# Convolution taps and softmax exponentials tied to later places in a hybrid decoder layer

## The chip, the cores and the metric

The kernel runs on one core of a Trainium2 chip. The metric is device microseconds from the start to the end of one execution; lower is better.

## The reference

One decoder layer, 256 tokens of width 1024, in fp32, up to the final norm:

```python
hn = rmsnorm(h, mix_norm_g[l])
conv_a, conv_b, q, k_c, v_c, ... = split(hn @ w_in[l])
y_conv = conformer_conv(conv_a, conv_b, ...)   # a*sigmoid(b), 31-tap causal depthwise conv, layernorm, silu
y_nsa  = nsa_mixer(q, k_c, v_c, ...)           # compressed, selected and window attention, gated
h = h + concat([y_conv, y_nsa]) @ w_out[l]
h = h + memory_attention(rmsnorm(h, ...), rmsnorm(mem, ...), ...)
h = h + peer(rmsnorm(h, ...), ...)             # product keys: top 16 of 128 x 128 experts, 8 heads
return rmsnorm(h, final_norm_g)
```

In `peer`, each token takes per head the 16 best of 16,384 experts, a softmax over their scores gives the gates, and the output is the sum over experts of gate x gelu(h . u) x v.

## The kernel before

**Engines.** PE (TensorE) multiplies. An fp32 product is made of three: each weight chunk of 128 x 1024 comes by DMA from SP's queue into `raw` (4 buffers), ACT rounds each half of it to `hi` (line 137), and DVE or POOL subtracts to get `lo` (line 138); lines 148 to 150 then multiply hi by the activations' high and low part, and lo by the high part, for 8 values of k: 24 matmuls per chunk. PE's instructions run in the order of the program text. The other engines' instructions were put in order by a list scheduler at build time; each engine works strictly through its own list. `tc.keep_in_program_order(t)`, which the change uses, forbids the scheduler to put instruction t ahead of anything written before it on the same engine; what is written behind t may still be moved ahead of it.

**First stretch (0 to 105 us).** Loop `for i in range(4)` projects the convolution's inputs, two weight chunks for each i (`pb`, `pa`). The first norm's scale is a sum over the channels (`r0`), put into a row by `r0.rows()` (matmul `sr_x`, line 224, then ACT's `rs_x`). `conv_in` scales, gates and writes `u[:, i]`, and appends the 31 taps of channel block i to a list; `conv(n)` takes n taps off the list and writes them into the program. One tap (lines 271 and 273) is one DVE instruction on 128 x 256, accumulating into `yc[:, i]`: 124 in all. Then come the compressed keys' and values' projections (`pkv`), the queries and keys (`pq`, with their rotation on DVE and ACT, `rope`), and the values (`pv`), with conv(3) after each chunk. Then PE works on the memory's keys (`pmk`, line 442), whose matmuls `fill` doles out as filler for the attention.

**Attention loop (`for n in range(18)`, 100 to 183 us).** Each n issues the scores of a unit of heads (`pss`), filler matmuls (`pmk`, then `pmv`), the transposes of unit n-2 (`ptt`), and conv(6). On DVE a unit is a row maximum (`amx`, lines 562 and 563), a reciprocal and a product (`asm`, 568 and 569) and a scaling (`ape`, 574). At n = 0 `cmp_keys` writes `kcT` (500, 501). At n = 12 `ln_mean` writes the remaining taps and adds up the four blocks into `lsum` (610 to 613); at n = 13 `ln_center` multiplies it with ones (`pmu`, 619) and subtracts (621).

**Experts (317 to 1107 us).** DVE works down a chain of top-16 searches (lines 901 to 953) for two halves of the tokens: scores, candidates, the softmax's inputs `ge` (928), and the experts' indices `ix` (953), which the gate matrices need. Beside it PE multiplies with all 128 chunks of u (`u_chunk`, result `pu`), ACT writes their gelu: the first J = 36 into `slA` (999), the others into `slB`. POOL splits the weights (`lo`) for i < J, DVE for the others. `choice_gates` at i = J - 12 = 24 has, for each half, the exponential of `ge` (ACT, 962; it needs another activation table than gelu, so a table load stands ahead of it, and another ahead of the next gelu), the sums `gs`, their reciprocal, and the product `gt` (964 to 967). `picked_out` transposes indices and gates at i = 30 to 35. From chunk 36 on, `gates4` (64 times) makes gate columns of four tokens on DVE and PE and multiplies them in (lines 1012 to 1024). Then line 1072 accumulates Y over all 128 chunks of v, from 759 us on.

Of the kernel before, what the change touches and what calls it, by code (L numbers as in the profile page):

```python
# [9 lines left out]
F32 = mybir.dt.float32  # L10
# [5 lines left out]
AF = mybir.ActivationFunctionType  # L16
ALU = mybir.AluOpType
# [3 lines left out]
P = 128  # L21
T = 256
D = 1024
KC = 8
# [68 lines left out]
def build(tc, A, out, dbg=None):  # L93
    nc = tc.nc
    V, S, G, PE = nc.vector, nc.scalar, nc.gpsimd, nc.tensor
# [17 lines left out]
    def Pm(name):  # L113
        return par[:, PC[name][0]:PC[name][1]]
# [28 lines left out]
    def wchunk(src, engs=None, width=P):  # L143

        return wsplit(wload(src), engs, width)
# [6 lines left out]
    def proj(ps, w, x, ks=range(KC)):  # L152
        for k in ks:
            mm3(ps, w[k], x[0][:, k], x[1][:, k], k == 0, k == KC - 1)
# [20 lines left out]
    def psum(w, name, tag="mm"):  # L175
        return pm.tile([P, 512], F32, name=name, tag=tag, bufs=4)[:, :w]
# [70 lines left out]
    hx = (hx_h, hx_l)  # L247
# [11 lines left out]
    u = ch.tile([P, 4, 30 + T], F32, name="u")  # L259
    V.memset(u[:, :, 0:30], 0.0)  # L260
    yc = ch.tile([P, 4, T], F32, name="yc")
    taps = []

    def conv(n):
        for _ in range(min(n, len(taps))):
            taps.pop(0)()

    def tap(i, j):
        w = Pm("conv_w")[:, i * TAPS + j:i * TAPS + j + 1]
        if j == 0:  # L270
            V.tensor_scalar(yc[:, i], u[:, i, 0:T], w, Pm("conv_b")[:, i:i + 1], op0=ALU.mult, op1=ALU.add)
        else:
            V.scalar_tensor_tensor(yc[:, i], u[:, i, j:j + T], w, yc[:, i], op0=ALU.mult, op1=ALU.add)  # L273

    def conv_in(i, pb, pa):
        tb = wk.tile([P, T], F32, name=f"tb{i}", tag="tb")
        V.tensor_mul(tb, pb, r0.row)
        th = wk.tile([P, T], F32, name=f"th{i}", tag="th")
        S.activation(th, tb, AF.Tanh, scale=0.5)
        ta = wk.tile([P, T], F32, name=f"ta{i}", tag="ta")  # L280
        V.scalar_tensor_tensor(ta, pa, 0.5, r0.row, op0=ALU.mult, op1=ALU.mult)
        V.scalar_tensor_tensor(u[:, i, 30:], th, 1.0, ta, op0=ALU.add, op1=ALU.mult)
        for j in range(TAPS):
            taps.append(lambda j=j: tap(i, j))

    pend = []
    for i in range(4):
        pb = psum(T, f"pb{i}")
        wb = wchunk(A["w_in_t"][2 * i]) if i else w0
        proj(pb, wb, hx, range(4))  # L290
        if i == 1:
            r0.sums()
        proj(pb, wb, hx, range(4, KC))
        wa = wchunk(A["w_in_t"][2 * i + 1], None)
        if i == 0:
            for k in range(KC):
                r0.add(xT[:, k])
            nc.sync.dma_start(con1, A["con"][:, 0:NCON1])
        pa = psum(T, f"pa{i}")
        proj(pa, wa, hx, range(6))  # L300
        if i == 1:
            r0.rows()
            conv_in(*pend)
        proj(pa, wa, hx, range(6, KC))
        if i == 0:
            pend = (i, pb, pa)
        else:
            conv_in(i, pb, pa)
        conv(6)
    nc.sync.dma_start(con2, A["con"][:, NCON1:])  # L310
    posi = wk.tile([P, T], I32, name="posi", tag="rt")
    nc.sync.dma_start(posi, A["pos"].partition_broadcast(P))
# [31 lines left out]
    for i in range(2):  # L344
        G.memset(KV[i], 0.0)
        ps = psum(T, f"pkv{i}")
        proj(ps, wchunk(A["w_in_t"][8 + i]), hx)
        kvT = wk.tile([P, T], F32, name=f"kvT{i}", tag="kvT")
        V.tensor_mul(kvT, ps, r0.row)
        kt = KV[i]  # L350
        S.activation(kt[0:64, 0, 0:T], kvT[0:64, :], AF.Copy)
        S.activation(kt[64:128, 1, 0:T - 1], kvT[64:128, 1:T], AF.Copy)
        nc.sync.dma_start(kt[64:128, 0, 0:T - 1], kvT[0:64, 1:T])
        nc.sync.dma_start(kt[0:64, 1, 0:T], kvT[64:128, :])
        V.tensor_copy(kt[:, 2, 0:32:2], Pm("cmp_pos")[:, 16 * i:16 * i + 16])
        conv(3)
    nc.sync.dma_start(w2, A["w2"])

    w1 = [mp.tile([P, 16, P], F32, name=f"w1_{i}", tag=f"w1_{i}") for i in range(2)]
# [31 lines left out]
    for i in range(6):  # L391
        dst = kraw[i] if i < 2 else qraw[:, i - 2]
        ps = psum(T, f"pq{i}")
        proj(ps, wchunk(A["w_in_t"][10 + i]), hx)
        V.tensor_mul(dst, ps, r0.row)
        if i >= 2:
            nc.sync.dma_start(w1[i // 2 - 1][:, 8 * (i % 2):8 * (i % 2) + 8], A["w1"][i // 2 - 1, :, 8 * (i % 2):8 * (i % 2) + 8])
        if i == 1:
            rm.sums()
        todo.append((i, dst))  # L400
        if i > 1:
            rope(*todo.pop(0))
        conv(3)


    vn = ch.tile([P, 2, 256], F32, name="vn")
# [1 line left out]
    for w in range(4):  # L408
        wc = wsplit(wload(A["w_in_v"][w], 560), (V, V), 280, 280)
        for j in range(2):  # L410
            k = 2 * w + j
            for hf in range(2):
                sl = slice(hf * P, (hf + 1) * P)
                PE.matmul(pv[hf], hx_h[:, k, sl], wc[j][0], start=(k == 0), stop=False)
                PE.matmul(pv[hf], hx_h[:, k, sl], wc[j][1], start=False, stop=False)
                PE.matmul(pv[hf], hx_l[:, k, sl], wc[j][0], start=False, stop=(k == KC - 1))
        if w % 2:
            rope(*todo[w // 2])
        if w == 1:
            rm.rows()  # L420
        conv(3)
    gate = ch.tile([P, 2, 8, 3], F32, name="gate")
    chalf = wk.tile([P, 2], F32, name="chalf", tag="bcol")
    V.tensor_scalar(chalf, r0.col, 0.5, None, op0=ALU.mult)
# [210 lines left out]
    for n in range(18):  # L635
        if n < 16:
            scores(*units[n])
        if n == 17:
            wc0 = wchunk(A["w_out"][0])
        fill(7 if n < 4 else 5 if n < 14 else 6)  # L640
        if n == 0:
            cmp_keys()
        if n == 1:
            cmp_values()
            cmp_scores(0)
        if n == 2:
            cmp_scores(1)
            prs = psum(512, "prsel", "at")
            for k in range(4):
                PE.matmul(prs[:, k * P:(k + 1) * P], C("rsel")[0:64, k * P:(k + 1) * P], vc2, start=True, stop=True)  # L650
            V.tensor_copy(vcp, prs.rearrange("p (a b) -> p a b", a=4))
        if n in (4, 5):
            cmp_transpose(n - 4)
        if n >= 6 and (n - 6) % 4 == 0:
            weighted((n - 6) // 4)
        if n >= 2:
            transposes(*units[n - 2])
        conv(6)
        if n == 12:
            lsum = ln_mean()  # L660
        if n == 13:
            ln_center(lsum)
        if n == 15:
            rc.sums()
        if n == 16:
            rc.rows()
            ln_out()
# [32 lines left out]
    for i in range(2, KC):  # L700
        ps = psum(T, f"pwo{i}")
# [118 lines left out]
    for i in range(2, KC):  # L820
        ps = psum(T, f"pmw{i}")
# [27 lines left out]
    for i in range(16):  # L849
        ps = psum(T, f"ppq{i}")  # L850
# [16 lines left out]
    hn_h = h2p.tile([P, KC, T], F32R, name="hn_h", tag="act_h")  # L867
    hn_l = h2p.tile([P, KC, T], F32R, name="hn_l", tag="act_l")
# [9 lines left out]
    pp = outer.enter_context(tc.tile_pool(name="pp", bufs=1, space=PSUM, **RW))  # L878
# [17 lines left out]
    for hf in range(2):  # L896
        top = tp.tile([P, 16, 16], F32, name=f"top{hf}", tag="top")
        tix = tp.tile([P, 16, 16], U32, name=f"tix{hf}", tag="tix")
        for hp in range(16):
            s = sco[hf][:, hp]  # L900
# [58 lines left out]
    def choice_gates():  # L959
        for hf in range(2):  # L960
            ge = picked[hf][2]
            S.activation(ge, ge, AF.Exp)
            gs = tp.tile([P, 8], F32, name=f"gs{hf}", tag="gs")
            V.tensor_reduce(gs, ge, axis=AX.X, op=ALU.add)
            V.reciprocal(gs, gs)
            gt = picked[hf][2] = tp.tile([P, P], F32, name=f"gt{hf}", tag=f"gt{hf}")
            V.tensor_tensor(gt.rearrange("p (k h) -> p h k", h=8), ge, gs.unsqueeze(2).to_broadcast([P, 8, 16]), op=ALU.mult)
            show(f"g_{hf}", gt)

    def picked_out(hf, j):  # L970

        sl = slice(hf * P, hf * P + P)
        pt = pp.tile([P, 512], F32, name=f"ptk{hf}{j}", tag="w", bufs=2)[:, 0:P]
        PE.transpose(pt, picked[hf][j], C("ident"))
        if j < 2:
            S.activation((i1T, i2T)[j][:, sl], pt, AF.Copy)  # L976
        else:
            S.activation(gTh[:, sl], pt, AF.Copy, scale=GSC)
            V.scalar_tensor_tensor(gTl[:, sl], pt, GSC, gTh[:, sl], op0=ALU.mult, op1=ALU.subtract)


    J = 36
    e1 = outer.enter_context(tc.tile_pool(name="e1", bufs=1, side="left", **RW))
    slA = e1.tile([P, J, T], F32, name="slA")
    tmp = outer.enter_context(tc.tile_pool(name="tmp", bufs=2, side="left", **RW))
# [1 line left out]
    V.tensor_copy(iota2, C("iota").unsqueeze(2).to_broadcast([P, P, 2]))  # L987

    def u_chunk(i):
        ps = pp.tile([P, 512], F32, name=f"pu{i}", tag="w" if i < J - 8 and i % 4 > 1 else "s", bufs=2)[:, 0:T]  # L990
        proj(ps, wchunk(A["u"][i], (G, G) if i < J else (V, V)), (hn_h, hn_l))
        return ps

    for i in range(J):
        if i == J - 12:
            choice_gates()
        if i >= J - 6:
            picked_out((i - J + 6) // 3, (i - J) % 3)
        S.activation(slA[:, i], u_chunk(i), AF.Gelu_apprx_tanh)
    tk_st.close()  # L1000
    e2 = outer.enter_context(tc.tile_pool(name="e2", bufs=1, side="right", **RW))
# [170 lines left out]
```

## Time and profile before

| | |
|---|---|
| median of 3 runs | 1117.01 us (1116.13 to 1117.02) |
| profiled execution | 1117.35 us, of which the span of the trace is 1115.6 |
| PE busy | 1069.5 us, 96% of the span, 7362 matmuls |
| DVE, ACT, POOL busy | 882.1 us (79%), 590.1 us (53%), 111.2 us (10%) |
| mean granted TensorE clock | 0.983 of full speed |
| chain that ended last | PE 87%, DVE 5%, issue 4%, POOL 2%, ACT 2% |

Times are counted from the span's start. A row of a timeline gives the start, the duration, the engine, the line, the operation with output<-inputs, and in brackets how long the engine had stood idle and whose end released it. A row that ends in x3 is three like instructions in a row, and its duration reaches from the first's start to the last's end. Durations overlap a little: an instruction's successor can start before its last result is written, so start-to-start distances are what a queue costs. "PEclk" or granted clock is the share of full speed (2.4 GHz) that TensorE was granted in a stretch; 0.5 is 1.2 GHz.

### The profile page before, as it was taken

To read this page: it belongs to the slowest core of one execution; us is meant where nothing else is said; L and a number is where in the kernel's file an instruction comes from. 1 tells how busy PE (TensorE), PEld (TensorE's weight loads), DVE (VectorE), ACT (ScalarE), POOL (GpSimd) and SP (SyncE) were. 2 spreads that over 40 slices of the span, in tenths; PEclk is the share of its full clock that TensorE was granted. 3 is DMA by queue.
4 is the path that set the end of the run, shared out by engine and by line. 5 is a ranking of instruction groups with operands and counts; after the bars stand their busy time and mean duration, and the time that the engine had idled before them with its cause. 6 is when DMAs were issued, how large, how long until landed. Compare 5 with 4: busy or idle time off the path is not lost.

```text
span 1115.6 us, 20623 instructions
## 1 busy us (share of the span) xinstructions
PE 1069.5 (96%) x7362; PEld 980.5 (88%) x7362; DVE 882.1 (79%) x2229; ACT 590.1 (53%) x1354; POOL 111.2 (10%) x86
## 2 busy tenths in 40 slices
PE   8889999999999849999999999999999999999997
PEld 7878778999999749999999999998888888888885
DVE  7998857988789995788899999996666666666665
ACT  5722456666446335566555555455555555555554
POOL 0000000000037749300000000000000000000000
PEclk9899999999999969999999999999999999999999
DMA  8633224625434415644545454456555556665662
GB/s 279 201 107 103 76 95 139 219 97 171 153 114 151 152 57 189 194 164 154 170 155 167 155 170 163 160 170 209 189 195 196 193 190 193 199 193 191 194 198 80
DMA packets 51687, 182.47 MB, mean 164 GB/s; under 512 B 5760, under 2 KB 6528, under 8 KB 51456
## 3 DMA queue, kind: packets, MB, share of 16 engines
q1 hardware_dynamic: 51296, 180.62, 49.8%
q8 instruction: 58, 0.95, 0.3%
q10 hardware_dynamic: 288, 0.52, 0.1%
q14 instruction: 45, 0.37, 0.1%
HBM read 179.81 MB, written 1.05 MB: 162 GB/s over the span
## 4 chain that ended last, share of the span: by engine, by line
PE 87%; DVE 5%; issue 4%; POOL 2%; ACT 2%; DMA 0%; SPq 0%; POOLq 0%; ACTq 0%; DVEq 0%
PE Y L1072 31%; PE pu L148 10%; PE pu L150 10%; PE pu L149 10%; PE pmk L442 3%; POOL lo L138 2%; PE pmv L458 2%; PE pw L1018 1%; PE ppq L148 1%; PE ppq L149 1%; PE ppq L150 1%; PE pw L1019 1%; DVE lo L138 1%; PE pmw L149 1%; PE pmw L148 1%
## 5 line engine op out<-in xcount | busy, mean ns | idle before, releaser
L137 ACT ACTIVATE hi<-raw 128x512 fp32r<-128x512 f32 x632 | 379.2, 623 | 175.8 <-PE pu L149 61.5
L138 DVE TENSOR_TENSOR lo<-raw,hi 128x512 fp32r<-128x512 f32 (+1 forms) x560 | 370.4, 683 | 26.3 <-ACT hi L137 20.0
L148 PE MATMUL pu<-hn_h,hi 128*128 128x256 f32 x1024 | 296.3, 289 | 18.2 <-ACT hi L137 18.2
L150 PE MATMUL pu<-hn_h,lo 128*128 128x256 f32 x1024 | 291.7, 285 | 2.7 <-POOL lo L138 2.7
L149 PE MATMUL pu<-hn_l,hi 128*128 128x256 f32 x1024 | 290.2, 283 | 0.0
L148 PEld LDWEIGHTS pu<-hn_h,hi 128*128 128x128 f32 x1024 | 197.0, 192 | 18.4 <-ACT hi L137 18.4
L150 PEld LDWEIGHTS pu<-hn_h,lo 128*128 128x128 f32 x1024 | 196.7, 192 | 5.3 <-POOL lo L138 5.1
L149 PEld LDWEIGHTS pu<-hn_l,hi 128*128 128x128 f32 x1024 | 197.1, 193 | 0.0
L1072 PE MATMUL Y<-hi,al 128*128 128x512 f32 x512 | 158.1, 389 | 0.0
L1072 PE MATMUL Y<-hi,ah 128*128 128x512 f32 x512 | 158.1, 389 | 0.0
L1072 PE MATMUL Y<-lo,ah 128*128 128x512 f32 x512 | 158.0, 389 | 0.0
L1072 PEld LDWEIGHTS Y<-hi,al 128*128 128x128 f32 x512 | 96.1, 188 | 19.9
L1072 PEld LDWEIGHTS Y<-lo,ah 128*128 128x128 f32 x512 | 96.1, 188 | 19.9
L1072 PEld LDWEIGHTS Y<-hi,ah 128*128 128x128 f32 x512 | 96.0, 188 | 20.0
L158 DVE TENSOR_TENSOR al<-slB,ah 128x256 fp32r<-128x256 f32 x92 | 39.1, 425 | 89.9 <-PE Y L1072 89.9
L138 POOL TENSOR_TENSOR lo<-raw,hi 128x512 fp32r<-128x512 f32 x72 | 103.7, 1476 | 36.5 <-ACT hi L137 36.4
L157 ACT ACTIVATE ah<-slB 128x256 fp32r<-128x256 f32 x92 | 38.5, 418 | 115.7 <-PE Y L1072 115.7
L1024 ACT ACTIVATE slB<-pw 128x364 f32<-128x364 f32 (+31 forms) x64 | 33.4, 522 | 64.7 <-DVE slB L1023 54.2
L273 DVE SCALAR_TENSOR_TENSOR yc<-u,par,yc 128x256 f32<-128x256 f32 x120 | 56.0, 478 | 0.3
L158 DVE TENSOR_TENSOR al<-slA,ah 128x256 fp32r<-128x256 f32 x36 | 15.3, 425 | 33.6 <-PE Y L1072 33.6
L1012 DVE TENSOR_TENSOR o<-iota,i1T 128x512 f16<-128x512 f16 x64 | 28.6, 448 | 12.7 <-ACT i1T L976 12.7
L157 ACT ACTIVATE ah<-slA 128x256 fp32r<-128x256 f32 x36 | 15.0, 418 | 44.1 <-PE Y L1072 43.0
(387 smaller groups left out, 1786.7 us busy)
## 6 DMA issues: line engine op xcount, KB each, us to landing
raw<-u SPq DMA_DIRECT2D x128, 512.0 KB, 3.4
raw<-v SPq DMA_DIRECT2D x128, 512.0 KB, 4.3
raw<-peer_w_q SPq DMA_DIRECT2D x16, 512.0 KB, 3.3
raw<-w_in_t SPq DMA_DIRECT2D x15, 512.0 KB, 4.3
raw<-w_mem_k SPq DMA_DIRECT2D x8, 512.0 KB, 3.4
raw<-w_mem_v SPq DMA_DIRECT2D x8, 512.0 KB, 3.4
raw<-w_out SPq DMA_DIRECT2D x8, 512.0 KB, 3.5
raw<-w_mem_q SPq DMA_DIRECT2D x8, 512.0 KB, 4.3
```

Source lines behind the costliest of these rows:

```text
L137: S.activation(hi, r, AF.Copy)
L138: (engs or (V, V))[q].tensor_sub(lo, r, hi.bitcast(F32))
L148: PE.matmul(ps, w[0], xh, start=start, stop=False)
L149: PE.matmul(ps, w[0], xl, start=False, stop=False)
L150: PE.matmul(ps, w[1], xh, start=False, stop=stop)
L157: S.activation(dst[0], src, AF.Copy)
L158: V.tensor_sub(dst[1], src, dst[0].bitcast(F32))
L273: V.scalar_tensor_tensor(yc[:, i], u[:, i, j:j + T], w, yc[:, i], op0=ALU.mult, op1=ALU.add)
L442: PE.matmul(ps, wr[:, k * P:(k + 1) * P], mg[:, k], start=(k == 0), stop=(k == KC - 1))
L1012: V.tensor_tensor(o1, i4, over_i(i1T), op=ALU.is_equal)
L1024: S.activation(slB[:, done - J:, n0:n0 + 4].rearrange("p i n -> p n i"), pw[:, :, done:], AF.Copy, scale=1.0 / GSC)
L1072: PE.matmul(Y[nh][c], lhs[:, sl], wc[c][t], start=False, stop=i == KEYS - 1 and lhs is a[1], skip_group_check=True)
```

## The change

It has two parts. **Convolution:** each tap is tied behind all that is written before it on DVE. The first norm's row and the gating of channel blocks 0 and 1 move from chunk i = 1 (after six values of k) to i = 2 (after four). `pb0` and `pa0` go to the PSUM tag "at", so that they live until then. Fewer taps are written in the first stretch (conv(4), conv(2)) and more in the attention loop (conv(7)). **Experts:** the exponentials are tied behind all that ACT has been given so far; J goes from 36 to 40, so that `choice_gates` stands at chunk 32 rather than 24; POOL splits chunks 0 to 33 (JG = 34) and DVE from 34 on; `picked_out` runs two per chunk at 37 to 39 rather than one at 30 to 35. The gate groups are spread over the chunks from 40 on, up to chunk 125, as before.

```diff
@@ tap
-            V.tensor_scalar(yc[:, i], u[:, i, 0:T], w, Pm("conv_b")[:, i:i + 1], op0=ALU.mult, op1=ALU.add)
+            t = V.tensor_scalar(yc[:, i], u[:, i, 0:T], w, Pm("conv_b")[:, i:i + 1], op0=ALU.mult, op1=ALU.add)
         else:
-            V.scalar_tensor_tensor(yc[:, i], u[:, i, j:j + T], w, yc[:, i], op0=ALU.mult, op1=ALU.add)
+            t = V.scalar_tensor_tensor(yc[:, i], u[:, i, j:j + T], w, yc[:, i], op0=ALU.mult, op1=ALU.add)
+        tc.keep_in_program_order(t)
@@ for i in range(4)
-        pb = psum(T, f"pb{i}")
+        pb = psum(T, f"pb{i}", "mm" if i else "at")
...
-        pa = psum(T, f"pa{i}")
-        proj(pa, wa, hx, range(6))
-        if i == 1:
+        pa = psum(T, f"pa{i}", "mm" if i else "at")
+        proj(pa, wa, hx, range(4))
+        if i == 2:
             r0.rows()
-            conv_in(*pend)
-        proj(pa, wa, hx, range(6, KC))
-        if i == 0:
-            pend = (i, pb, pa)
+            for p in pend:
+                conv_in(*p)
+        proj(pa, wa, hx, range(4, KC))
+        if i < 2:
+            pend.append((i, pb, pa))
         else:
             conv_in(i, pb, pa)
-        conv(6)
+        conv(4)
@@ after each chunk of pkv, of pq and of pv
-        conv(3)
+        conv(2)
@@ for n in range(18)
-        conv(6)
+        conv(7)
@@ choice_gates
-            S.activation(ge, ge, AF.Exp)
+            tc.keep_in_program_order(S.activation(ge, ge, AF.Exp))
@@ experts
-    J = 36
+    J = 40
+    JG = 34
@@ u_chunk
-        ps = pp.tile([P, 512], F32, name=f"pu{i}", tag="w" if i < J - 8 and i % 4 > 1 else "s", bufs=2)[:, 0:T]
-        proj(ps, wchunk(A["u"][i], (G, G) if i < J else (V, V)), (hn_h, hn_l))
+        ps = pp.tile([P, 512], F32, name=f"pu{i}", tag="w" if i < J - 6 and i % 4 > 1 else "s", bufs=2)[:, 0:T]
+        proj(ps, wchunk(A["u"][i], (G, G) if i < JG else (V, V)), (hn_h, hn_l))
@@ for i in range(J)
-        if i == J - 12:
+        if i == J - 8:
             choice_gates()
-        if i >= J - 6:
-            picked_out((i - J + 6) // 3, (i - J) % 3)
+        if i >= J - 3:
+            for j in range(2):
+                picked_out((2 * (i - J + 3) + j) // 3, (2 * (i - J + 3) + j) % 3)
```

Line numbers of the changed kernel are one to four higher than those of the kernel before.

ACT's order in the experts, before, around the first exponential (`hi` is a rounding, `slA` a gelu; the row at line 999 with `pu_4522` is the gelu of chunk 3):

```order
L137 ACTIVATE hi_4597<-raw_4595 128x512
L137 ACTIVATE hi_4601<-raw_4595 128x512
L999 ACTIVATE slA<-pu_4486 128x256
L137 ACTIVATE hi_4633<-raw_4631 128x512
L137 ACTIVATE hi_4637<-raw_4631 128x512
L999 ACTIVATE slA<-pu_4522 128x256
L962 ACT_TABLE_LOAD
L962 ACTIVATE ge_4175<-ge_4175 128x128
L137 ACTIVATE hi_4669<-raw_4667 128x512
```

The second half's exponential stands in the same way behind the gelu of chunk 14. ACT's order now, around both (`pu_5530` is chunk 31; `raw_5651` is chunk 34's weights):

```order
L1003 ACTIVATE slA<-pu_5494 128x256
L137 ACTIVATE hi_5653<-raw_5651 128x512
L137 ACTIVATE hi_5657<-raw_5651 128x512
L1003 ACTIVATE slA<-pu_5530 128x256
L964 ACT_TABLE_LOAD
L964 ACTIVATE ge_4175<-ge_4175 128x128
L964 ACTIVATE ge_4367<-ge_4367 128x128
L137 ACTIVATE hi_5689<-raw_5687 128x512
L1003 ACT_TABLE_LOAD
L1003 ACTIVATE slA<-pu_5578 128x256
```

The exponentials moved from behind chunks 3 and 14 to behind chunk 31 and the roundings of chunk 34, and share two table loads instead of four.

DVE's order now at the end of the searches (`ix_4403` is the last of the chain, `raw_5651` again chunk 34's weights; before, no `lo` stood here, and chunk 36's came behind the first rows of the gate groups):

```order
L953 TENSOR_TENSOR ohx_4397<-ohx_4397 128x512
L953 TENSOR_TENSOR ohx_4397<-ohx_4397 128x256
L955 TENSOR_TENSOR ix_4403<-ohx_4397 128x128
L138 TENSOR_TENSOR lo_5654<-raw_5651,hi_5653 128x512
L138 TENSOR_TENSOR lo_5658<-raw_5651,hi_5657 128x512
L966 TENSOR_REDUCE gs_5567<-ge_4175 128x8
L967 RECIPROCAL gs_5567<-gs_5567 128x8
L969 TENSOR_TENSOR gt_5570<-ge_4175,gs_5567 128x8x16
L138 TENSOR_TENSOR lo_5690<-raw_5687,hi_5689 128x512
```

The first weights that DVE splits now stand behind its last search, with the sums of the gates behind them; the two sets of gs and gt rows stood inside the searches before.

DVE's order now at the end of the taps in the attention loop (`raw_1999` and `raw_2028` are the first two weight chunks of `w_out`):

```order
L576 TENSOR_SCALAR ape_1816<-ape_1816,asm_1817 128x256
L273 SCALAR_TENSOR_TENSOR yc<-u,par,yc 128x256 x2
L138 TENSOR_TENSOR lo_2002<-raw_1999,hi_2001 128x512
L273 SCALAR_TENSOR_TENSOR yc<-u,par,yc 128x256
L138 TENSOR_TENSOR lo_2006<-raw_1999,hi_2005 128x512
L273 SCALAR_TENSOR_TENSOR yc<-u,par,yc 128x256 x9
L138 TENSOR_TENSOR lo_2031<-raw_2028,hi_2030 128x512
L273 SCALAR_TENSOR_TENSOR yc<-u,par,yc 128x256
L138 TENSOR_TENSOR lo_2035<-raw_2028,hi_2034 128x512
L273 SCALAR_TENSOR_TENSOR yc<-u,par,yc 128x256 x6
L614 TENSOR_TENSOR lsum_1804<-yc 128x256
L615 TENSOR_TENSOR lsum<-lsum,lsum_1804 128x256
```

Between the second `kcT` row and this `lsum` row there are now 92 taps (before 36), 24 more rows of the attention's units, and four `lo` of `w_out` (before none). Ahead of the last rotation of the first stretch there are 30 taps (before 57), and between that and `kcT` two (before 31).

## Rows read from the trace of the kernel before

**Rows 1.** The page: parts 1 and 5 (busy, mean ns | idle before, releaser).
```profile
PE 1069.5 (96%) x7362; PEld 980.5 (88%) x7362; DVE 882.1 (79%) x2229; ACT 590.1 (53%) x1354; POOL 111.2 (10%) x86
...
L148 PE MATMUL pu<-hn_h,hi 128*128 128x256 f32 x1024 | 296.3, 289 | 18.2 <-ACT hi L137 18.2
...
L138 DVE TENSOR_TENSOR lo<-raw,hi 128x512 fp32r<-128x512 f32 (+1 forms) x560 | 370.4, 683 | 26.3 <-ACT hi L137 20.0
```

**Rows 2.** Timeline of ACT, 340 to 404 (start us, us, engine line op [idle before <-releaser]).
```profile
340.31 0.36 ACT L999 ACTIVATE slA<-pu 128x256 f32<-128x256 f32 x1
...
343.19 0.36 ACT L999 ACTIVATE slA<-pu 128x256 f32<-128x256 f32 x1
...
348.80 0.31 ACT L962 ACTIVATE ge<-ge 128x128 f32<-128x128 f32 x1 [3.95 <-DVE ge L928]
...
403.06 0.31 ACT L962 ACTIVATE ge<-ge 128x128 f32<-128x128 f32 x1 [23.77 <-DVE ge L928]
```

**Rows 3.** Timeline of PE, 384 to 410.
```profile
385.46 0.28 PE L150 MATMUL pu<-hn_h,lo 128*128 128x256 f32 x1
...
403.94 0.58 PE L148 MATMUL pu<-hn_h,hi 128*128 128x256 f32 x1 [18.20 <-ACT hi L137]
...
406.15 0.41 PE L150 MATMUL pu<-hn_h,lo 128*128 128x256 f32 x1
...
408.85 0.31 PE L148 MATMUL pu<-hn_h,hi 128*128 128x256 f32 x1
```

**Rows 4.** Windows: us; busy of PE, PEld, DVE, ACT, POOL; PEclk, DMA share, GB/s.
```profile
25.00:85.00 60.00, 50.83 (x360) 48.81 (x359) 56.39 (x155) 30.41 (x66) 0.00 (x0) 0.90 0.51 165
...
108.55:145.02 36.47, 36.47 (x201) 29.03 (x199) 32.50 (x111) 16.57 (x61) 0.00 (x0) 1.00 0.25 82
...
720.00:740.00 20.00, 20.00 (x184) 19.83 (x183) 20.00 (x45) 10.79 (x30) 0.00 (x0) 1.00 0.47 154
```

**Rows 5.** Timeline of PE, 43 to 90.
```profile
45.27 0.58 PE L150 MATMUL pkv<-hx_h,lo 128*128 128x256 f32 x1 [4.63 <-DVE lo L138]
...
84.87 5.34 PE L442 MATMUL pmk<-mg,raw 128*128 128x256 f32 x24
```

**Rows 6.** Timeline of DVE, 89 to 138, taps.
```profile
90.00 2.85 DVE L273 SCALAR_TENSOR_TENSOR yc<-u,par,yc 128x256 f32<-128x256 f32 x7
...
135.36 1.53 DVE L273 SCALAR_TENSOR_TENSOR yc<-u,par,yc 128x256 f32<-128x256 f32 x3
```

**Rows 7.** Timelines of DVE and PE, 108 to 165.
```profile
108.55 0.24 DVE L501 TENSOR_SCALAR kcT<-pkc,par 64x16 f32<-64x16 f32 x1
...
144.59 0.43 DVE L613 TENSOR_TENSOR lsum<-lsum,lsum 128x256 f32<-128x256 f32 x1
...
164.75 0.60 PE L619 MATMUL pmu<-lsum,ones 128*128 128x256 f32 x2
```

**Rows 8.** Timeline of POOL, 330 to 440.
```profile
336.94 7.92 POOL L138 TENSOR_TENSOR lo<-raw,hi 128x512 fp32r<-128x512 f32 x6 [0.93 <-ACT hi L137]
...
349.71 33.50 POOL L138 TENSOR_TENSOR lo<-raw,hi 128x512 fp32r<-128x512 f32 x22 [4.85 <-ACT hi L137]
```

**Rows 9.** Timeline of DVE, 403 to 467.
```profile
403.47 0.28 DVE L942 SCALAR_TENSOR_TENSOR pd<-pu,pu 128x128 f32<-128x128 uint32 x1
...
410.67 1.37 DVE L942 SCALAR_TENSOR_TENSOR pd<-pu,pu 128x128 f32<-128x128 uint32 x1
...
422.56 1.50 DVE L967 TENSOR_TENSOR gt<-ge,gs 128x128 f32<-128x128 f32 x1
...
430.65 1.27 DVE L953 TENSOR_TENSOR ix<-ohx 128x128 f32<-128x128 f16 x1
...
444.58 2.75 DVE L1012 TENSOR_TENSOR o<-iota,i1T 128x512 f16<-128x512 f16 x2 [12.65 <-ACT i1T L976]
...
466.13 0.42 DVE L1012 TENSOR_TENSOR o<-iota,i1T 128x512 f16<-128x512 f16 x1
```

**Rows 10.** Timeline of ACT, 429 to 470.
```profile
461.94 0.36 ACT L999 ACTIVATE slA<-pu 128x256 f32<-128x256 f32 x1
```

More of the change, by code (lines that the diff above doesn't have):

```diff
@@ L402, in build @@
             rope(*todo.pop(0))
-        conv(3)
+        conv(2)
     vn = ch.tile([P, 2, 256], F32, name="vn")
@@ L420, in build @@
             rm.rows()
-        conv(3)
+        conv(2)
     gate = ch.tile([P, 2, 8, 3], F32, name="gate")
```

## The prediction

> **What bounds the kernel now.** I read the page's busy shares first: PE is busy for 1069.5 of 1115.6 us, so a change can only win what PE loses at its few stops, and can lose whatever new stop it makes [rows 1]. The costliest stop is in the same part of the page: one wait of 18.2 us of the u multiplication for a rounding on ACT [rows 1]. The timeline of ACT tells why the rounding was late. ACT stood still for 3.95 us ahead of the first exponential and for 23.77 us ahead of the second, both for DVE's `ge`, with the roundings of later chunks queued behind [rows 2]. PE ran out of rounded weights at 385.46, resumed at 403.94, and its matmuls took 0.41 us instead of 0.28 until 408.85 [rows 3]. That is half-speed work, 1.2 instead of 2.4 GHz: 15 matmuls in 4.91 us, of which 0.8 went to two waits for POOL, against 1.8 at 0.12 each (24 take 2.88, the distance of two gelus [rows 2]). The aftermath of a long stop costs 2.3 us.
>
> Then the windows, for the stretches in which the taps lie. From 25 to 85 us DVE is busy for 56.39 of 60 us and PE for 50.83, at a mean clock of 0.90: DVE sets the pace there [rows 4]. One of PE's waits shows it, 4.63 us for a `lo` [rows 5]. From 108.55 to 145.02 PE never stops, and DVE works 32.50 of 36.47 us [rows 4]. There DVE is ahead: `lsum` ends at 145.02, and `pmu` needs it at 164.75 [rows 7].
>
> **The convolution, first stretch.** Ahead of the last rotation 27 taps go (57 before, 30 now, by the order). Where blocks alternate, a tap costs 2.85 / 7 = 0.41 us of DVE's queue [rows 6], so DVE loses 27 x 0.41 = 11 us, up to the point that releases `pmk`, the start of PE's next work, at 84.87 [rows 5]. Not all of it comes forward: pinned taps can't fill holes any more, and a wait for the positions' sine and cosine, now hidden by taps, can move to the next split. With 3.6 us of holes now and PE alone needing some 46 us at full speed, I take 9.5, bounds 5 and 11. The first norm's row goes a chunk later, with its tanh and gating; its DVE rows are the same ones, and it has another chunk's work in front of it. Costed at nothing: DVE's queue behind it sets the end either way. If that cover went, PE would wait for a split once more, as in the row of 4.63 us.
>
> **The convolution, attention loop.** What was taken off comes back here. Between the second `kcT` row and `lsum` there are 56 more taps, 24 more rows of units, and four splits. Before, 111 instructions took 36.47 us, with 32.50 busy [rows 4]. The units' rows cost 32.50 / 111 = 0.29 each, 7.0 together; the splits 4 x 0.683 = 2.7 [rows 1]. The taps are now in one fixed sequence, block by block, so neighbours depend on each other. Alternating with other work they cost 0.41; three in a row took 1.53, so 0.51 each [rows 6]. The order has both kinds, alternating rows and runs of six and nine. The lower end, with 0.41 and all holes filled, since a late DVE finds its inputs ready: 108.55 + 32.5 + 23 + 2.7 + 7 = 173.7. The upper, with 0.51 and all holes kept: 108.55 + 36.5 + 28.6 + 2.7 + 7 = 183.3. I take the middle, 178.4, because the order has both kinds and holes go only once DVE is late. In the frame of before, `pmu` is due at 164.75 [rows 7]. So **a new wait of 13.6 us** (9 to 18.6) arises there, or partly at transposes that wait for the same queue, and 2.3 behind it for the half speed. The 20 us of slack that `lsum` had are used up and more. Queued behind the late `lsum` on DVE are `pmu`'s subtraction and the second norm, which therefore keep their distance. The weights of `w_out` whose splits moved ahead arrive in time: DMA is busy 0.25 of this stretch [rows 4].
>
> A rule bears on the 0.41 and 0.51. The Trainium skill, page "VectorE: DVE Perf Modes", section "The DRAIN you can't avoid", says that a flush of the pipe stands behind every DVE operation, and that chained copies took the same time with and without waits between them (an operation that nothing holds may start earlier, it adds). By its copies all taps would cost alike, and at 0.51 the wait would be at its upper end; the two rows above disagree, since seven taps of different blocks went through faster.
>
> Stretch one, summed: -9.5 + 13.6 + 2.3 = **+6.4**.
>
> **The exponentials.** ACT's waits go: by the order both stand behind chunk 31's gelu, some 28 chunks after chunk 3's at 343.19, so at about 343.2 + 28 x 2.88 = 424, and the second `ge` is ready by then (below). Undisturbed, PE goes on at 2.88 per chunk: chunk 33 would end at 343.19 + 30 x 2.88 = 429.6 and chunk 35 at 435.35, where it ended at 461.94 before [rows 10]. That is -26.6. It holds the 18.2 and the half speed, and also stretches in which POOL set the pace.
>
> Two prices stand against it. First, **POOL no longer pauses**, and DVE works beside it. One operation of the search took 0.28 us while POOL stood still and 1.37 at POOL's side [rows 9]: 1.09 more. In POOL's two pauses DVE passed 18 such instructions in all (7 around 349, 5 from 392 to 402, 6 around 403; max searches are not touched). Without pauses 12 of them, 13.1 us, come before the second `ge`, which moves from 402.77 to 415.9. POOL itself needs 68 splits now: 36 were done by 383.21, which without the 4.85 of its first pause is 378.4 [rows 8]; 32 more at 33.50 / 22 = 1.52 end at 427.1. Second, **chunk 34 is split by DVE behind its last search**. That search ended at 431.92 [rows 9]. From the second `ge` it had 29.15 us to go, less some 2 for the gates' rows, which leave the chain (the largest, 1.50 us, is [rows 9]). By 427.1, six contended rows later (6.5 us), 4.6 of these 27.1 are done; the 22.5 left hold 15 instructions that POOL no longer slows, each cheaper by 2.75 / 2 - 0.42 = 0.96 [rows 9]. So it ends at 427.1 + 22.5 - 14.4 = 435.2, and the first split at 435.9. PE wants it at 430.0, two matmuls into chunk 34. That is a wait of 5.9, and 2.3 of half speed. Net: -26.6 + 5.9 + 2.3 = **-18.4**. Bounds: no wait, -26.6, and no relief, below.
>
> Here too there is a rule, and it speaks against this change. The Trainium skill, page "SBUF — State Buffer", section "Who interferes with whom", says that DVE and GpSimd share a port pair under an exclusive lock: the later one is blocked until the other's instruction is through. By it a late-comer would lose the rest of a running split, half of one on average, and the sum would be that of rival (b); the row of 1.37, a whole split longer, puts it higher.
>
> Costed at nothing: two table loads fewer (ACT is busy 53% [rows 1]); transposes of indices two per chunk (the same six); the gate groups over 85 chunks instead of 89, and DVE's four further splits (chunks 34, 35), 2.7 us. Late in this phase DVE is full, 20.00 of 20 us, but so is PE, which does not wait [rows 4]. If that cover failed, it would cost up to those 2.7 us.
>
> **Sum.** 1117.35 (the profiled execution, span 1115.6 and 1.75 around it, 0.34 above the median) + 6.4 - 18.4 = 1105.35, called **1105 us**. Its own bounds, from the ends above: 1095 and 1114.
>
> **Rivals.** (a) DVE keeps up in the attention loop: `pmu` does not wait, since its 20 us of slack cover the taps. Then 1117.35 - 9.5 - 18.4 = 1089. For it: 19.7 us of slack and 4 of holes; against it: 23 us of taps and 9.7 of other rows go in. (b) DVE's chain is in time for chunk 34. A search row that comes while a split runs may have to wait for the rest of it alone, on average half of 7.92 / 6 = 1.32 [rows 8], so 0.66 instead of 1.09: 18 x 0.43 = 8 us earlier than the forecast for the chain, no wait, 1105.35 - 8.2 = 1097. The lock of the page named above would have it so. Against it: POOL's splits follow without gaps, and 1.37 against 0.28 is nearly a whole one. (c) **Slower**: the chain gets no relief, because POOL, held up in its turn by DVE's two-input instructions, still works when the last search runs. Then the chain ends at 431.9 - 2 + 18 x 1.09 = 449.5, the first split at 450.2, PE waits for 20.2, as long as the wait that went, and the time is 1105.35 + 14.3 = 1119.7. It is slower from a chain end of 449 us on. Against it: 22 splits of POOL's took 1.52 each, also beside a busy DVE. (d) The edit does nothing, as where a scheduler had put things there anyway; the order excludes it for taps and exponentials alike.
>
> **Chances.** A measurement of this kernel tells 0.2%, 2.2 us, from no change: 1114.8 to 1119.2. Forecast 0.62; (a) 0.14, (b) 0.14, (c) 0.07; something that eats both gains without a loss 0.03. The range leaves out (c) and the far part of (a): 1090 to 1115. Faster takes the forecast, (a) and (b): 0.90; same 0.04 (the rest, and a mild (c)); slower 0.06.
>
> **What would show it.** In the profile after: `pmk` starts near 75 us; `pmu` comes some 14 us later than its neighbours allow, with an idle time released by DVE's `lsum`; both exponentials follow chunk 31's gelu without a wait; the 18.2 us wait of `pu` for ACT is gone, and one of about 6 us for DVE's `lo` stands near chunk 34; the search instructions near the old pauses take 1.3 us; Y starts near 747.5. A `pmk` start near 85 makes the first term wrong; no wait at `pmu`, the second; a wait of 15 us or more at chunk 34, the third.

## The result, and the profile after

The changed kernel takes **1102.57 us** (median of 4 runs, 1101.85 to 1102.73) against 1117.01 (1116.13 to 1117.38) before: a ratio of 0.9871, 95% interval 0.9853 to 0.9888. The forecast was 1105, its range 1090 to 1115. The profiled execution took 1101.85, with a span of 1100.1.

The page of the changed kernel, parts 1 and 5, the lines that answer to [rows 1]:

```profile
PE 1062.4 (97%) x7361; PEld 976.2 (89%) x7362; DVE 878.9 (80%) x2229; ACT 587.6 (53%) x1349; POOL 101.5 (9%) x82
...
L148 PE MATMUL pu<-hn_h,hi 128*128 128x256 f32 x1024 | 295.9, 289 | 0.0
...
L150 PE MATMUL pu<-hn_h,lo 128*128 128x256 f32 x1024 | 290.4, 284 | 2.3 <-DVE lo L138 2.3
...
L138 POOL TENSOR_TENSOR lo<-raw,hi 128x512 fp32r<-128x512 f32 x68 | 93.8, 1407 | 12.0 <-ACT hi L137 9.2
```

PE's busy time fell by 7.1 us for the same work: the mean granted clock rose from 0.983 to 0.989. Its share rose from 96 to 97%. The 18.2 us of idle time ahead of `pu` for ACT are 0.0. What is new stands in the view of PE's waits (us in total, times, longest):

```profile
PE pmu L621 <- ACT hi L137: 14.7, 1, 14.7
PE pq L150 <- DVE lo L138: 4.7, 2, 4.2
PE pu L150 <- DVE lo L138: 2.3, 1, 2.3
```

So a wait of 18.2 us went, and one of 14.7 came. The starts of five pieces of work show where (us from the span's start, from the views of single tiles):

| | pmk | pmu | first slA | Y | end |
|---|---|---|---|---|---|
| before | 84.9 | 164.8 | 336.0 | 759.5 | 1115.6 |
| changed | 76.0 | 170.8 | 342.5 | 744.0 | 1100.1 |
| convolution part alone | 75.7 | 170.5 | 342.6 | 768.0 | 1124.0 |
| experts' part alone | 84.8 | 164.6 | 335.8 | 737.1 | 1093.2 |
| taps in the gap (below) | 76.4 | 157.6 | 327.8 | 727.9 | 1084.0 |

Up to `pmk` the change wins 8.9 us. Between `pmk` and `pmu` it loses 14.9, and the experts start 6.5 us later. From there to Y it wins 22.0 (423.5 to 401.5). Behind Y nothing changed.

PE's timeline in the changed kernel around the first two (line 621 answers to 619 in [rows 7], 444 to 442 in [rows 5]):

```profile
75.97 2.32 PE L444 MATMUL pmk<-mg,raw 128*128 128x256 f32 x10
...
155.43 0.60 PE L586 MATMUL ptt<-con,ape 128*128 128x128 f32 x4
170.77 1.19 PE L621 MATMUL pmu<-lsum,ones 128*128 128x256 f32 x2 [14.74 <-ACT hi L137]
```

And DVE's in the same stretch:

```profile
99.66 0.24 DVE L503 TENSOR_SCALAR kcT<-pkc,par 64x16 f32<-64x16 f32 x1
...
160.46 4.64 DVE L273 SCALAR_TENSOR_TENSOR yc<-u,par,yc 128x256 f32<-128x256 f32 x9
...
170.20 0.42 DVE L615 TENSOR_TENSOR lsum<-lsum,lsum 128x256 f32<-128x256 f32 x1
```

`pmk` starts at 75.97 instead of 84.87. PE is done with what stands ahead of `pmu` at about 156 and begins `pmu` at 170.77, 0.15 us after `lsum` ends at 170.62. The row names ACT's rounding as the releaser, but that is only what ended last on record by the trace; what `pmu` reads is `lsum`. DVE needed 71.0 us from `kcT` to the end of `lsum`, where it had needed 36.5 [rows 4]. Nine taps in a row took 4.64 us there, 0.515 each.

In the experts, ACT's timeline:

```profile
430.37 0.37 ACT L1003 ACTIVATE slA<-pu 128x256 f32<-128x256 f32 x1
430.75 1.28 ACT L964 ACT_TABLE_LOAD   x1
432.04 0.51 ACT L964 ACTIVATE ge<-ge 128x128 f32<-128x128 f32 x2
```

Both exponentials run behind chunk 31's gelu, without a wait; before, 3.95 and 23.77 us [rows 2]. The timelines of POOL, DVE and PE:

```profile
343.47 86.09 POOL L138 TENSOR_TENSOR lo<-raw,hi 128x512 fp32r<-128x512 f32 x60 [0.42 <-ACT hi L137]
```

```profile
418.04 0.98 DVE L930 TENSOR_TENSOR ge<-best 128x128 f32<-128x128 f32 x1
418.94 0.22 DVE L933 TENSOR_SCALAR late<-pos 128x128 f32<-128x128 uint32 x1
419.08 1.31 DVE L938 TENSOR_SCALAR pu<-pos 128x128 uint32<-128x128 uint32 x1
420.31 0.21 DVE L939 TENSOR_SCALAR pu<-pos 128x128 uint32<-128x128 uint32 x1
420.56 1.34 DVE L944 SCALAR_TENSOR_TENSOR pd<-pu,pu 128x128 f32<-128x128 uint32 x1
...
430.57 0.28 DVE L944 SCALAR_TENSOR_TENSOR pd<-pu,pu 128x128 f32<-128x128 uint32 x1
...
437.16 0.29 DVE L955 TENSOR_TENSOR ix<-ohx 128x128 f32<-128x128 f16 x1
437.37 1.29 DVE L138 TENSOR_TENSOR lo<-raw,hi 128x512 fp32r<-128x512 f32 x2
```

```profile
435.57 0.28 PE L149 MATMUL pu<-hn_l,hi 128*128 128x256 f32 x1
438.11 0.58 PE L150 MATMUL pu<-hn_h,lo 128*128 128x256 f32 x1 [2.26 <-DVE lo L138]
438.49 0.41 PE L148 MATMUL pu<-hn_h,hi 128*128 128x256 f32 x1
```

POOL's splits run without a pause, 60 in 86.09 us, 1.435 each. DVE's last `ix` ends at 437.45, its first split (two rows in 1.29) follows at once, and PE, which had asked for it since 435.85, goes on at 438.11 after 2.26 us, at half speed (0.41 us a matmul) at first. While POOL works, one search instruction (line 944) takes 1.34 us; behind POOL's end at 429.56 it takes 0.28 again.

### The profile page after: what moved, and what is told of

Read it like the earlier page. It is cut to its first block, busy times and chain, and to the rows that moved or that the text cites. A ratio compares the mean times of both kernels' runs of the same rounds, so it can differ in the third digit from the quotient of the medians.

```text
span 1100.1 us, 20606 instructions
## 1 busy us (share of the span) xinstructions
PE 1062.4 (97%) x7361; PEld 976.2 (89%) x7362; DVE 878.9 (80%) x2229; ACT 587.6 (53%) x1349; POOL 101.5 (9%) x82
## 4 chain that ended last, share of the span: by engine, by line
PE 82%; DVE 14%; DMA 2%; ACT 1%; issue 1%; SPq 0%; DVEq 0%; ACTq 0%
PE Y L1076 31%; PE pu L148 9%; PE pu L150 8%; PE pu L149 8%; PE pmk L444 3%; PE pmv L460 2%; PE pw L1022 1%; PE ppq L148 1%; PE ppq L149 1%; PE ppq L150 1%; PE pw L1023 1%; DMA raw<-w_in_t 1%; DVE lo L138 1%; DVE ohx L953 1%; DVE yc L273 1%; DVE ohx L951 1%
## 5 line engine op out<-in xcount | busy, mean ns | idle before, releaser
L1076 PE MATMUL Y<-hi,ah 128*128 128x512 f32 x512 | 158.2, 389 | 0.0
L138 POOL TENSOR_TENSOR lo<-raw,hi 128x512 fp32r<-128x512 f32 x68 | 93.8, 1407 | 12.0 <-ACT hi L137 9.2
L1028 ACT ACTIVATE slB<-pw 128x348 f32<-128x348 f32 (+31 forms) x64 | 32.5, 507 | 71.3 <-DVE slB L1027 59.7
L148 PE MATMUL ppq<-gx_h,hi 128*128 128x256 f32 x128 | 37.3, 292 | 0.0
```

What stands on the lines that cost most here:

```text
L138: (engs or (V, V))[q].tensor_sub(lo, r, hi.bitcast(F32))
L148: PE.matmul(ps, w[0], xh, start=start, stop=False)
L1028: S.activation(slB[:, done - J:, n0:n0 + 4].rearrange("p i n -> p n i"), pw[:, :, done:], AF.Copy, scale=1.0 / GSC)
L1076: PE.matmul(Y[nh][c], lhs[:, sl], wc[c][t], start=False, stop=i == KEYS - 1 and lhs is a[1], skip_group_check=True)
```

## The experiments

The diffs are against the changed kernel, or against the kernel named. Times are medians; ratios are against the kernel before, run beside each kernel on the same chip (medians 1118.1 to 1119.1 us there).

### Each part alone

The gates' code as before, the convolution as changed (**conv_alone**); and the reverse (**gates_alone**): each is the hunks of the one part alone. In **untied_exps** only the tie goes:

```diff
-            tc.keep_in_program_order(S.activation(ge, ge, AF.Exp))
+            S.activation(ge, ge, AF.Exp)
```

> The convolution part alone, gates as before. My theory (the two parts add up; the taps cost more in the attention loop than they give back ahead of it): the wait of some 14.7 us at pmu stays as in the changed kernel, pmk starts near 76, the first slA comes 6.5 us later than before, and the 18.2 us wait of pu for ACT is back: 1117.0 + 6.5 = 1123.5 us. Rival (the convolution part is neutral, and the wait at pmu is made up for later): 1117 us, within 2.

> The experts' part alone, convolution as before. My theory: no wait at pmu; the 18.2 us wait gone; a wait of 2 to 3 us for DVE's lo at chunk 34; 1117.0 - 22 = 1095 us, so faster than both kernels. Rival (the gain needs the shifted start of the experts): 1103 us or more.

> The changed kernel with the exponentials not tied. By the order the scheduler puts them behind the gelu of chunks 3 and 14 again. My theory (the tie carries the whole gain of the experts' part): the wait of about 18 us of pu for ACT is back, 1102.6 + 22 = 1124 us. Rival (the move of J, of JG and of choice_gates carries it): 1103 to 1107 us.

Measured: **conv_alone** 1126.3 us, ratio 1.0079 (1.0052 to 1.0105); **gates_alone** 1095.0, 0.9795 (0.9772 to 0.9818); **untied_exps** 1126.3, 1.0074 (1.0051 to 1.0098). PE's waits in the three, in this order:

```profile
PE pu L148 <- ACT hi L137: 18.2, 1, 18.2
PE pmu L621 <- ACT hi L137: 14.7, 1, 14.7
```

```profile
PE pu L150 <- DVE lo L138: 1.9, 1, 1.9
```

```profile
PE pu L148 <- ACT hi L137: 18.2, 1, 18.2
PE pmu L621 <- ACT hi L137: 14.7, 1, 14.7
```

The parts add up: their spans differ from before by +8.4 and -22.4, together -14.0, and the whole change by -15.5. The convolution part makes the kernel slower by itself, and the experts' part alone beats the whole change. Without the tie, J, JG and the place of `choice_gates` bring nothing: the 18.2 us wait is back whole, since the scheduler puts the exponentials where they were. The time is 2 to 3 us above the 1123.5 and 1124 expected, in both kernels with that wait. The kernel before, run beside them, took 1119.1 instead of 1117.0. In the traces, conv_alone needs 1.9 us more from the first `slA` to Y than the kernel before, with a new wait of 1.4 for `ptk`; in the untied one 1.3 is a later start of `pmk`.

### The wait at pmu

**taps_in_gap** writes part of the taps ahead of the attention loop, still tied:

```diff
     fill(12)
+    conv(12)
...
     for i in range(2):
...
+        conv(6 if i else 10)
...
-        conv(7)
+        conv(5)
```

DVE's busy time in the changed kernel, windows with the columns of [rows 4], says why there:

```profile
80.00:90.00 10.00, 10.00 (x69) 9.33 (x67) 2.67 (x11) 1.06 (x3) 0.00 (x0) 1.00 0.30 105
90.00:100.00 10.00, 10.00 (x61) 8.64 (x59) 4.26 (x18) 2.47 (x9) 0.00 (x0) 1.00 0.26 83
```

> The changed kernel with 28 of the loop's taps written ahead of the loop instead (12 behind the first 12 filler matmuls, 10 and 6 behind the two compressed keys' gelu chains) and conv(5) in the loop; by the order 54 taps instead of 32 stand ahead of kcT, and no lo of w_out ahead of lsum. My theory (DVE is idle there, 2.67 and 4.26 of 10 us busy at 80 to 100, and the wait at pmu is nothing but the queue of taps behind kcT): lsum 22 x 0.45 + 4 x 0.68 = 12.6 us earlier, the wait at pmu 14.7 - 12.6 = 2 us, time 1102.6 - 13 = 1090 us. Rival (the wait at pmu has another cause, such as a rounding on ACT that the trace names, or the chain of dependent taps): 1100 us or more.

Measured: **1085.6 us**, ratio 0.9710 (0.9687 to 0.9733), faster than both kernels. The same windows, and `pmu`:

```profile
80.00:90.00 10.00, 10.00 (x68) 9.33 (x67) 7.77 (x21) 0.83 (x2) 0.00 (x0) 1.00 0.31 105
90.00:100.00 10.00, 10.00 (x61) 8.80 (x61) 7.00 (x24) 2.07 (x8) 0.00 (x0) 1.00 0.23 69
```

```profile
157.57 0.67 PE L623 MATMUL pmu<-lsum,ones 128*128 128x256 f32 x2 [1.10 <-DVE lsum L617]
```

The taps fill the idle time, the wait is 1.1 us, and now the trace names `lsum` as its end. The 8.5 us that `pmk` comes earlier are kept. The estimate was 4 us too high; 3 of them are the half-speed work behind the wait, some 2 us, which it left out, and a wait that shrank by 13.6 instead of 12.6.

**untied_taps** takes only the tie away, with all numbers of `conv()` as changed:

```diff
-        tc.keep_in_program_order(t)
```

> The changed kernel with the taps not tied, all numbers of conv() as changed. By the order 67 taps stand ahead of kcT instead of 32, 36 ahead of the last rotation instead of 30, and no lo of w_out ahead of lsum. My theory (the tie, not the numbers, puts the taps behind kcT and makes the wait at pmu): lsum comes 35 x 0.46 + 2.7 = 19 us earlier, the wait of 14.7 us and its half-speed aftermath of about 2 are gone, sr_c's wait of 1.0 is back, the first stretch gives back 6 x 0.41 = 2.5: 1102.6 - 14.7 - 2 + 1 + 2.5 = 1089 us. Rival (the later numbers make it): 1102 us, with the wait at pmu above 10 us.

Measured: 1086.9 us, ratio 0.9720 (0.9705 to 0.9735). `lsum` and `pmu`, from DVE's and PE's timelines:

```profile
149.93 0.42 DVE L614 TENSOR_TENSOR lsum<-lsum,lsum 128x256 f32<-128x256 f32 x1
```

```profile
156.72 0.60 PE L620 MATMUL pmu<-lsum,ones 128*128 128x256 f32 x2
```

`lsum` starts 20 us earlier than in the changed kernel, and `pmu` doesn't wait. So it is the tie, and not the numbers, that puts the taps behind `kcT`: in the loop `conv()` is first called behind `kcT`, and a tied tap can't be moved up into the idle time ahead. The early gain does not need the tie: `pmk` starts at 76.8 here.

**mixed_taps** keeps the tie, and deals the remaining taps out over the channel blocks, so that neighbours don't depend on each other:

```diff
+    left = [[t for t in taps if t[0][0] == c] for c in range(4)]
+    taps[:] = [b[k] for k in range(TAPS) for b in left if k < len(b)]
     for n in range(18):
```

(the list's entries carry their block and number for this).

> The changed kernel with the taps that are left at the loop's start dealt out block by block in turn, so that neighbours never depend on each other; still tied. My theory: only taps that stand directly behind each other pay for the dependence (0.51 instead of 0.41); the trace of the changed kernel has 25 such pairs among its 92 taps, so lsum comes 25 x 0.1 = 2.6 us earlier: 1100 us, wait at pmu about 12 us. Rival (the dependence costs every tap 0.1, across other rows too): 9 us earlier, 1094 us.

Measured: 1099.3 us, ratio 0.9840 (0.9824 to 0.9856), with this wait:

```profile
PE pmu L621 <- DVE lsum L615: 8.4, 1, 8.4
```

The time is near the first expectation. The wait is 6.4 us shorter: `lsum` ends 4.2 us earlier (166.46 instead of 170.62), and PE is done with what stands ahead of `pmu` 2.2 us later (158.2 instead of 156.0), of which 1.2 is a later start of `pmk`. From `kcT` to the end of `lsum` DVE needs 5.3 us less. Start-to-start distances of DVE's rows, summed over the taps with idle stretches over 0.15 us taken out, give 40.4 us for 92 taps in the changed kernel, 0.44 each, and 36.5 for 92 here, 0.40 each: the dependence costs 3.9 us. In the changed kernel the 27 taps that have another right behind them took 0.51 each on average, the other 65 took 0.41, so neighbours pay, and not every tap, as the rival had it. By the order, two `lo` fewer stand ahead of `lsum` here, 1.2 us more. The time fell by only 3.3: from `pmu` to the output projection PE needed 1.4 us more. That is longer half speed behind the wait: the twelve `pmv` matmuls there took 5.12 us instead of 3.84, and the granted clock was 0.50 from 166.6 to 172, where the changed kernel had 0.50 from 170.8 to 174 and 0.73 in the two us behind. Why it lasted longer is not shown.

### The wait at chunk 34

Three kernels move POOL's last chunk, from taps_in_gap on: **gap_jg30** (`JG = 30`), **gap_jg36** (`JG = 36`), and **gap_tie34** (`JG = 36`, `choice_gates` at `i == J - 6`).

> The kernel with taps in the gap (1085.6 us), and POOL splits chunks 0 to 29 only. It tests where the wait at chunk 34 comes from. My theory: POOL ends 8 x 1.435 = 11.5 us earlier, the rest of the search runs without it and ends some 7.7 us earlier (the excess of the eight rows that were slowed after that point in the changed kernel), but chunk 30 is wanted 11.5 us earlier than chunk 34: the wait of 2.3 us becomes 2.3 + 11.5 - 7.7 = 6 us, time 1089 to 1090 us. Rival (no relief: POOL does not slow the tail of the search): wait 13 us or more, 1096 us or more. Rival (the split does not wait for the search): no wait, 1083 us.

> The kernel with taps in the gap (1085.6 us), and POOL splits chunks 0 to 35. My theory: POOL ends 4 x 1.435 = 5.7 us later, which slows four or five more rows of the search by 1.1 each, so it ends some 5 us later; chunk 36 is wanted 5.8 us later than chunk 34: the wait of 2.3 us becomes 1 to 1.5 us, time 1084 to 1085 us. Rival (POOL no longer slows the tail): wait gone with its half-speed chunk, 1082 us. Rival (POOL slows all of the tail): 1088 us or more.

> The kernel with taps in the gap (1085.6 us), POOL splitting chunks 0 to 35 (as in the run with 36, 1087.5 us) and choice_gates at chunk 34. By the order the first lo of chunk 36 stands directly behind the last ix again, where the run with 36 had the six rows of gs and gt (1.8 us) between. My theory (the wait there is the end of DVE's queue, row by row): the wait of 2.4 us becomes 0.6, time 1084 to 1085.5 us. Rival (it is POOL's longer work, not the six rows): wait 2 us or more, 1087 us.

Measured: **gap_jg30** 1092.0 us, ratio 0.9766 (0.9751 to 0.9781); **gap_jg36** 1087.5, 0.9725 (0.9711 to 0.9738); **gap_tie34** 1085.6, 0.9712 (0.9698 to 0.9726). DVE's last `ix` in taps_in_gap, then in gap_jg30 with its first splits and PE's wait there:

```profile
422.43 0.29 DVE L957 TENSOR_TENSOR ix<-ohx 128x128 f32<-128x128 f16 x1
```

```profile
415.38 0.29 DVE L957 TENSOR_TENSOR ix<-ohx 128x128 f32<-128x128 f16 x1
415.59 4.43 DVE L138 TENSOR_TENSOR lo<-raw,hi 128x512 fp32r<-128x512 f32 x7
```

```profile
416.33 0.58 PE L150 MATMUL pu<-hn_h,lo 128*128 128x256 f32 x1 [5.82 <-DVE lo L138]
```

With POOL ended four chunks earlier the search ends 7.05 us earlier by the clock. The experts start 0.9 us later in this kernel; counted from each kernel's first `slA` (327.8 and 328.7) it is 7.96 (7.7 expected), and the wait is 2.26 + 11.5 - 7.96 = 5.8, as measured (6 expected). That shows both terms: POOL slows the tail of the search, and the first split waits for its end. The time is 2 us above the 1089 to 1090 expected: 0.9 is the later start, and the rest is about the half speed behind the wait (granted clock 0.50 from 416.33 to 420), which the expectation left out. In taps_in_gap no half speed follows, though PE waits as long as in the changed kernel:

```profile
423.38 0.39 PE L150 MATMUL pu<-hn_h,lo 128*128 128x256 f32 x1 [2.26 <-DVE lo L138]
```

The windows behind the two waits (columns of [rows 4]), first in the changed kernel and then in taps_in_gap, show a granted clock of 0.50 and of 1.00:

```profile
438.11:441.00 2.89, 2.89 (x13) 2.89 (x14) 2.75 (x9) 0.57 (x1) 0.00 (x0) 0.50 0.45 126
```

```profile
423.30:426.00 2.70, 2.62 (x22) 2.62 (x23) 2.56 (x9) 0.63 (x1) 0.00 (x0) 1.00 0.39 108
```

Why the clock fell in one and not in the other is open. From the first `slA` to Y taps_in_gap needs 400.1 us and the changed kernel 401.5, so the half speed there costs 1.4. In gap_jg36 the search ends 4.5 us later, 4.0 counted from the first `slA` (5 expected):

```profile
426.92 0.29 DVE L957 TENSOR_TENSOR ix<-ohx 128x128 f32<-128x128 f16 x1
427.13 0.28 DVE L968 TENSOR_REDUCE gs<-ge 128x8 f32<-128x128 f32 x1
...
428.96 4.42 DVE L138 TENSOR_TENSOR lo<-raw,hi 128x512 fp32r<-128x512 f32 x7
```

There the wait was 2.4 us instead of 1 to 1.5, since the scheduler had put the gates' six rows, 1.8 us, between the last `ix` and the split. The time is 2.5 us or more above the 1084 to 1085 expected, because half speed stands behind this wait too (mean granted clock 0.63 from 430 to 434). With these rows behind the split (gap_tie34) PE waits

```profile
428.83 0.38 PE L150 MATMUL pu<-hn_h,lo 128*128 128x256 f32 x1 [0.89 <-DVE lo L138]
```

0.89 us instead of 2.37, as expected to 0.3. The time is that of taps_in_gap all the same, within 1 us: from the first `slA` to Y it needs 398.7 us instead of 400.1, which is the shorter wait, but in its profiled execution `pmk` began 1.1 us later. The two can't be told apart.

### Where the tie stands, and the first norm's row

Two more from taps_in_gap: **gap_tie24** has `choice_gates` at `i == 24`; **gap_row_early** has the first norm's row, `conv_in` of blocks 0 and 1 and the PSUM tags as before.

> The kernel with taps in the gap (1085.6 us), with choice_gates at chunk 24 instead of 32, still tied. My theory (the tie only helps where ACT gets to it after the second ge): ACT arrives some 9 to 10 us ahead of the second ge and waits, PE has three rounded chunks in hand and stops for 4 to 5 us, loses some 2 at half speed, and the wait of 2.3 us at chunk 34 goes in return, with its half speed: 1087 to 1090 us, and a wait of pu for ACT's hi in the trace. Rival (where it is tied does not matter as long as it is one place): 1085.6 us, no such wait.

> The kernel with taps in the gap (1085.6 us), with the first norm's row and the gating of blocks 0 and 1 back at chunk i = 1, and pb0, pa0 back in their old PSUM tag. By the order 34 taps instead of 30 stand ahead of the last rotation. My theory (the fewer taps bring the 9 us of the first stretch; the row's move is worth next to nothing, though sr_x's wait of 2 us is back): pmk starts at 76.4 + 1.6 to 3, time 1086 to 1089 us. Rival (the row's move brings most of it): pmk at 82 or later, 1092 us or more.

Measured: **gap_tie24** 1093.2 us, ratio 0.9785 (0.9767 to 0.9804); **gap_row_early** 1087.5, 0.9723 (0.9705 to 0.9740). ACT's timeline and POOL's in gap_tie24:

```profile
393.43 1.28 ACT L966 ACT_TABLE_LOAD   x1
394.72 0.31 ACT L966 ACTIVATE ge<-ge 128x128 f32<-128x128 f32 x1
402.53 0.31 ACT L966 ACTIVATE ge<-ge 128x128 f32<-128x128 f32 x1 [7.50 <-DVE ge L932]
```

```profile
403.44 1.27 POOL L138 TENSOR_TENSOR lo<-raw,hi 128x512 fp32r<-128x512 f32 x1 [8.50 <-ACT hi L137]
405.65 21.49 POOL L138 TENSOR_TENSOR lo<-raw,hi 128x512 fp32r<-128x512 f32 x13 [0.95 <-ACT hi L137]
```

The place matters: ACT waits for the second `ge`, 7.5 us, and PE stops, for 2.2 us for ACT and 1.7 in all for POOL (4 to 5 expected). It cost 7.6 us instead of 1.4 to 4.4; 6.7 of these lie between the first `slA` and Y. I had the wait at chunk 34 go in return; but POOL stood idle for 8.5 us as well and ended 12 us later than in taps_in_gap, its splits slowed the search's tail for longer (it ends 4.9 us later, counted from the first `slA`), and 1.7 us of the wait remained. Half speed stands behind the first stop (mean granted clock 0.62 from 404 to 408), and none behind the last (1.00 from 430 to 437).

In gap_row_early the waits of PE ahead of `pmk` that differ from taps_in_gap (4.7 for `pq`, none for `sr_x`) are

```profile
PE pq L150 <- DVE lo L138: 3.6, 2, 2.8
PE sr_x L224 <- DVE dg_x L218: 2.0, 1, 2.0
```

`sr_x` waits again, `pq` for less, and `pmk` starts at 78.7, 2.3 us later than in taps_in_gap, four taps more ahead of it included. Kernels with one order up to `pmk` start it anywhere from 75.7 to 77.5 (see the last section), so the row's move with these taps is worth between 1.2 and 3.0 us. Without it 6.2 of the 8.9 us remain, so the fewer taps bring most of the first gain.

## Why the prediction was right, and where it was off

The time and its signs came out by the steps as put, in the frame of before where a clock time is compared. The profiled execution was 3.5 us faster than forecast (1101.85 and 1105.35), and that is the experts' term.

- **First stretch**: -9.5 forecast, -8.9 measured at `pmk`. The cause, 27 taps fewer ahead of the last rotation, holds for most of it: 6.2 remain without the row's move (gap_row_early). That move had been costed at nothing and is worth 1 to 3, with four taps.
- **Attention loop**: a wait of 13.6 forecast, 14.74 measured; `lsum` at 178.4 forecast, 170.62 + 8.9 = 179.5 measured. The middle held partly by compensation, which is luck. A tap cost 0.44 on average, less than the 0.46 I took, while the holes did not fill: stretches of idle time over 0.15 us add up to 5.3 us between `kcT` and `lsum`, 3.5 before, and I had taken half of them as filled. The aftermath, 2.3, came to 2.0 (18.0 us from `pmu` to the output projection before, 19.0 now, with `sr_c`'s wait of 1.0 gone). That the wait is the queue of tied taps is shown: filling the gap ahead or taking the tie away removes it.
- **Experts**: -18.4 forecast, -22.0 measured. The mechanisms held, the tie too (untied_exps, gap_tie24). **The mis-sized term is POOL beside the search**: I charged 1.09 us to each of 18 instructions. Of these 12 were slowed, ten by 0.7 to 1.1 us, a `CAST` (line 912) by 2.0 and another (990) by 0.3; the other six by less than 0.1. The timeline above shows a pattern: 0.22, 1.31, 0.21, 1.34. A short conversion right behind a slowed instruction gets through. So the second `ge` came at 418.04 - 6.54 = 411.5, not 415.9. POOL was also faster than taken, 1.435 per split instead of 1.52, and ended at 423.0 instead of 427.1. Both together put the end of the search at 437.45 - 6.54 = 430.9 instead of 435.2, and the wait at chunk 34 at 2.26 instead of 5.9; the half speed behind it cost 1.4 instead of 2.3. The relief of the tail held: I took 0.96 us for each instruction, and the 13 search rows behind POOL's end are 0.93 shorter on average than the same rows of the first half, which ran beside POOL.
- **The sum's bounds**: 1095 and 1114 do not come out of the ends of the terms, which give 1091 and, without rival (c), 1115. The range of 1090 to 1115 covers both.
- **Rivals**: (a) `pmu` waits, so the slack did not cover the taps. (b) was half right: the search was slowed by less than I took, but still too late for chunk 34. With the lock of the Trainium skill, page "SBUF — State Buffer", section "Who interferes with whom", the rows agree in kind: most slowed instructions are longer by 0.7 to 1.1 us, up to most of a split, but not each one that could be is slowed, and the 2.0 of the one `CAST` is more than a split of 1.435. (c) fell with the relief.
- **What was costed at nothing**: the late phase stayed free of waits with DVE full, and behind Y both kernels need 356.1 us.

## What to carry to other kernels

An instruction tied to its place can't be moved up into idle time ahead of it, so where a tied instruction is *written* must be where the engine is idle: the same tie cost 15 us behind `kcT` and 1 in the gap before it. Here the taps did not need it at all: without it the kernel takes 1086.9 us. An instruction that waits for a long chain on another engine belongs behind the work that others need from its engine meanwhile: the exponentials cost an 18 us stop ahead of the chain's end, and none behind it. A change of two parts is worth running part by part: here one part gave 22 us, and the other took some 8 of them back.

## What the runs showed that was not expected

Beside POOL's splits, DVE's short conversions (`TENSOR_SCALAR` on 128 x 128) took either 0.21 or 1.31 us; the two right behind a slowed instruction in the rows above took 0.21 and 0.22. Waits of about the same length were followed by half speed in some kernels and not in others: 2.26 us in the changed kernel and 2.37 in gap_jg36 were, 2.26 in taps_in_gap and 1.68 in gap_tie24 were not. The first stretch, with one order of instructions, put the start of `pmk` anywhere from 75.7 to 77.5 us in nine kernels, so differences of about 1 us between whole runs say nothing; the distance from the first `slA` to Y is the better measure there.
